# Seven block products for 20 of 22 up pairs in a split-precision FFN, with DMA-made weight sums in three buffers and tile addresses set by the kind of product

## The chip, the cores and the metric

The kernel runs on one core of a Trainium2 chip. The metric is the device time of one execution in microseconds (us), lower is better. A core has a matrix engine (TensorE, PE in the profile; its weight loads are listed as PEld), a vector engine (VectorE, DVE), an activation engine (ScalarE, ACT), a general engine (GpSimd, POOL) and a sync engine (SyncE, SP). They run their own instruction streams and meet through semaphores. Data lies in on-chip memory of 128 partitions, matmul results go to accumulation banks, and DMA queues move data; SP and POOL issue the DMAs spoken of here. "L398" is line 398 of the kernel before.

## The reference, cut to what matters

512 positions, width 1024, two layers. Layer 0 mixes tokens by causal pooling and a short convolution, layer 1 by gated linear attention; each layer then has a gated FFN with a convolution, and it is there that most of the change lies:

```python
def conv_ffn(h, w_up, conv_w, conv_b, w_down):
    u, v = jnp.split(h @ w_up, 2, axis=-1)          # 2816 channels each
    u = causal_dwconv(u, conv_w, conv_b)            # 3 taps over positions
    return (jax.nn.gelu(u, approximate=False) * v) @ w_down

def reference(x, ...):
    for l in range(DEPTH):                          # DEPTH = 2
        hn = rmsnorm(x, mix_norm[l])
        if l % 2 == 0:
            h = hn @ ab_w_in[i]
            ...                                     # pooling and short convolution
            y = jnp.concatenate([ya, yb], axis=-1) @ ab_w_out[i]
        else:
            y = gla_mixer(hn @ gla_w_in[i], ...) @ gla_w_out[i]
        x = x + y
        x = x + conv_ffn(rmsnorm(x, ffn_norm[l]), ffn_w_up[l], ffn_conv_w[l], ffn_conv_b[l], ffn_w_down[l])
    return rmsnorm(x, final_norm)
```

Inputs and output are float32.

## The kernel before

**Layout and precision.** Channels lie on the 128 partitions, the 512 positions along a row. Every float32 operand of a product is cut into a high and a low part by `split` (L136 on ACT makes the high part, L137 on DVE the low one), and every product is made in three passes: high by high, high by low, low by high. The normalized activations are held as eight tiles `xh[k]` and eight `xl[k]`. Weights come by DMA into raw tiles of 128x1024 (pool `wp`, four buffers of kind `raw`), and the parts into pool `wsp` (kinds `hi` and `lo`, four buffers each). For most weights `fetch` does load and split, one block ahead of use; `accumulate` (L219) then runs 8 matmuls of 512 columns for each pass.

**The stages.** In order: the input projection of layer 0 (pu, pc, px, pb by the program's names) and its mixer, the output projection abo, FFN up, FFN down (dn); then layer 1: a projection with the activations as the stationary operand (vg, L757 to L759, 256 columns), q, k and r, the attention, the output projection go, FFN up, FFN down. The last block of the last FFN down is made in two halves of 256 columns.

**FFN up** has 22 pairs in each layer; a pair is 128 channels of u and the 128 channels of v that they gate. `UP_KINDS` says how each pair is made:

- P, `plain`: two plain products, 2 x 3 passes x 8 = 48 matmuls of 512 columns (L398). The factor `rs` of the norm is multiplied in afterwards (L339). There are 6 P pairs per layer, at places 0, 1, 7, 13, 20 and 21.
- S, `seven`: the pair is seen as a 2x2 block product (u and v by the two halves of the 1024 inputs; those by the two halves of the 512 positions) and made with seven products in place of eight: p1 to p7, each 3 passes x 4 = 12 matmuls of 256 columns (L474), 84 in all, into the banks stx, sty and stz. There are 16 S pairs per layer.

The seven products need sums of blocks. On the activation side `mix_tokens` makes them once per layer (L341 to L360; the last of its additions is L352, and the parts are called th and tl). On the weight side each S pair makes them anew. The row of weights of a pair in memory is four quarters of 512: v.k1, v.k2, u.k1, u.k2.

- `load` issues three DMAs together, 12 units of the plan before the pair's start: L418 on SP brings v.k1 and v.k2 to a raw tile (raw left); L421 on SP brings u.k1 twice into a tile of kind `sum` (two buffers); L422 on POOL adds v.k1 to its first and u.k2 to its second half, with a DMA that accumulates. `load_right` (L426 on SP) brings u.k2 to the second half of another raw tile (raw right).
- `prep_a` splits raw left (a1). `prep_b` makes s2 (L443, DVE) from the sum's second half and v.k1, splits it (sh, sl), and makes a further difference, here called C (L445, DVE), from v.k2 and s2 into the first half of raw right. `prep_c` splits the sum (s31), `prep_d` raw right (a2).
- The products use them in this order: p1 and p2 read a1, p6 reads s2, p5 and p7 read s31, p4 and p3 read a2 (`LAYOUT`). On PE the p4 and p3 of a pair run among the products of the next one: p1, p2, p4 of the pair before, p6, p3 of the pair before, p5, p7.
- DVE and ACT take the results out of the banks (L483, L492, L505, L511, L516, L517), convolve over positions (`conv3`: L328 on ACT, L329 and L332 on DVE), and ACT applies the gelu.

**What sets the order.** `ffn_up` collects all its steps as events with a time in units (`at`): an S pair takes 7.0 units of this plan, a P pair 7.7 (`PERIOD`), and the sorted events are run. The framework then orders the instructions on each engine by its own estimates and inserts the semaphores: an instruction waits for the tiles that it reads and for the readers of the memory that it writes. SP's and POOL's issues go down their queues in their own order, and an issue that waits holds the ones behind it.

**Where tiles lie.** Single tiles of 128x512 come out of the pool `big` (`slot`, 46 buffers): u, v, the convolution's accumulators, s2, sh, sl, the gelu's results, y_h and y_l (parts of what abo and go read), vt (the attention's values) and mh and ml (parts of what FFN down reads). `xh` and `xl` are eight tiles each of 512 + 8 elements, of which 512 are used; the other tiles are 512 or 1024 elements with no gaps. The diagonal matrices of the norm (L265, DVE) feed matmuls (L276, L277) that spread the norm's factor; on PE they stand directly behind the first P pair, among the first products of the second pair.

Of the kernel before, what the change touches and what calls it, by code (L numbers as in the profile page):

```python
# [7 lines left out]
F32 = mybir.dt.float32  # L8
F32R = mybir.dt.float32r
I32 = mybir.dt.int32  # L10
AF = mybir.ActivationFunctionType
ALU = mybir.AluOpType

P = 128
T = 512
D = 1024
# [12 lines left out]
VG_COLS = (272, 256, 256, 256)  # L29
VG_K = ((3, 3, 2), (4, 4), (4, 4), (4, 4))  # L30
WBLK = 1024
NBIG = 46
AHEAD = 1
H = T // 2
HK = KD // 2
QUARTER = HK * P
UP_KINDS = "PPSSSSSPSSSSSPSSSSSSPP"
TILE_ORDER = (0, 4, 1, 5, 2, 6, 3, 7)
LAYOUT = {"p1": 0, "p2": 1, "p6": 3, "p5": 5, "p7": 6, "p4": 9, "p3": 11}
PERIOD = {"S": 7.0, "P": 7.7}  # L40
# [16 lines left out]
def trunk_kernel(ctx, tc, xT, cols, w_ab, w_pool, w_abo, w_vg, w_qkr, w_g2, w_go, w_up, w_dn, outT):  # L57
# [2 lines left out]

    cp = ctx.enter_context(tc.tile_pool(name="cp", bufs=1))
    big = ctx.enter_context(tc.tile_pool(name="big", bufs=NBIG))
    wp = ctx.enter_context(tc.tile_pool(name="wp", bufs=4))
    wsp = ctx.enter_context(tc.tile_pool(name="wsp", bufs=4))
    hp = ctx.enter_context(tc.tile_pool(name="hp", bufs=5))
    sp = ctx.enter_context(tc.tile_pool(name="sp", bufs=2))
# [1 line left out]

    def slot(dt=F32, name="s"):
        return big.tile([P, T], dt, tag="s", name=name)  # L70

    def half(name):
        return hp.tile([P, H], F32, tag="h", name=name)
# [4 lines left out]
    xall = cp.tile([P, KD * T], F32, tag="x", name="xall")  # L78
    x3 = xall.rearrange("p (k t) -> p k t", k=KD)
    x = [xall[:, k * T : (k + 1) * T] for k in range(KD)]  # L80
    xh = [cp.tile([P, T + 8], F32R, tag=f"xh{k}", name=f"xh{k}")[:, :T] for k in range(KD)]
    xl = [cp.tile([P, T + 8], F32R, tag=f"xl{k}", name=f"xl{k}")[:, :T] for k in range(KD)]
    colt = cp.tile([P, NCOLS], F32, tag="cols", name="colt")

    def col(name, i=0):
# [4 lines left out]
    for g in range(2):  # L90
        lead.append((
            wp.tile([P, WBLK], F32, tag="raw", name="raw_lead")[:, :D],
            wsp.tile([P, WBLK], F32R, tag="hi", name="hi_lead")[:, :D],
            wsp.tile([P, WBLK], F32R, tag="lo", name="lo_lead")[:, :D],
        ))

    def lead_load(g, part):
# [14 lines left out]
    for k in range(3, KD):  # L112
        x_load(k)

    ones = cp.tile([P, P], F32, tag="ones", name="ones")
    V.memset(ones, 1.0)
    ones_r = cp.tile([P, P], F32R, tag="ones_r", name="ones_r")
    V.tensor_copy(ones_r, ones)
    warm_in = sp.tile([P, 1], F32, tag="warm", name="warm_in", bufs=1)
    S.activation(warm_in, ones[:, 0:1], AF.Sqrt)  # L120
    warm = ps.tile([P, T], F32, tag="ps", name="warm")
# [17 lines left out]
    def weight_order():  # L139
        for g in range(2, 4):  # L140
            yield w_ab[g], KD, P
        for j in range(4):
            for b in (8 + j, 12 + j, 4 + j):
                yield w_ab[b], KD, P
        for j in TILE_ORDER:
            yield w_abo[j], KD, P
        for l in range(2):
            for j in range(NF):
                if UP_KINDS[j] == "P":
                    yield w_up[l, j, :, :D], KD, P  # L150
                    yield w_up[l, j, :, D:], KD, P
            for j in range(KD):
                k0 = 0
                for kt in DOWN_K:
                    yield w_dn[l, j, :, k0 * P : (k0 + kt) * P], kt, P
                    k0 += kt
            if l == 0:
                off = 0
                for n, ks in zip(VG_COLS, VG_K):
                    for kt in ks:  # L160
                        yield w_vg[:, off : off + kt * n], kt, n
                        off += kt * n
                for h in range(HEADS):
                    yield w_qkr[h], KD, P
                    yield w_qkr[4 + h], KD, P
                for i in range(8):
                    yield w_qkr[8 + i], KD, P
                for j in TILE_ORDER:
                    yield w_go[j], KD, P
# [5 lines left out]
    def fetch():  # L175
        nxt = next(order, None)
        if nxt is None:
            return
        fetched[0] += 1
        src, kt, n = nxt  # L180
        m = kt * n
        raw = wp.tile([P, WBLK], F32, tag="raw", name="raw")[:, :m]
        hi = wsp.tile([P, WBLK], F32R, tag="hi", name="hi")[:, :m]
        lo = wsp.tile([P, WBLK], F32R, tag="lo", name="lo")[:, :m]
        nc.sync.dma_start(raw, src)
        split(hi, lo, raw)
        ready.append([t.rearrange("p (k n) -> p k n", k=kt) for t in (hi, lo)])
# [172 lines left out]
    def ffn_up(l, rs, mixed):  # L360
# [12 lines left out]
        }  # L373
        ms = [None] * NF
        events = []

        def at(t, fn):
            events.append((t, len(events), fn))
# [33 lines left out]
        def seven(j, base):  # L412
            w, b, q = {}, {}, {}

            def load():
                src = w_up[l, j]
                w["raw", 0] = wp.tile([P, WBLK], F32, tag="raw", name="raw")
                nc.sync.dma_start(w["raw", 0], src[:, :D])  # L418
                s31 = w["s31"] = wp.tile([P, WBLK], F32, tag="sum", name="s31", bufs=2)
                s3 = s31.rearrange("p (a n) -> p a n", a=2)  # L420
                nc.sync.dma_start(s3, src[:, None, D : D + QUARTER].broadcast_to([P, 2, QUARTER]))  # L421
                G.dma_start(s3, src.rearrange("p (a n) -> p a n", a=4)[:, 0:4:3, :], accum_op=ALU.add)  # L422

            def load_right():
                w["raw", 1] = wp.tile([P, WBLK], F32, tag="raw", name="raw")
# [1 line left out]

            def parts(name, src, wide=True):
                if wide:
                    h = wsp.tile([P, WBLK], F32R, tag="hi", name="hi")  # L430
                    lo = wsp.tile([P, WBLK], F32R, tag="lo", name="lo")
                else:
                    h, lo = slot(F32R, "sh"), slot(F32R, "sl")
                split(h, lo, src)
                w[name] = (h, lo)

# [2 lines left out]

            def prep_b():  # L440
                r, c, s31 = w["raw", 0], w["raw", 1], w["s31"]
                s2 = slot(name="s2")
                V.scalar_tensor_tensor(s2, s31[:, QUARTER:], -1.0, r[:, :QUARTER], ALU.mult, ALU.subtract)  # L443
                parts("s2", s2, False)
                V.tensor_tensor(c[:, :QUARTER], r[:, QUARTER:], s2, ALU.subtract)  # L445
# [4 lines left out]
            def prep_d():  # L450
                parts("a2", w["raw", 1])

            at(base - 12, load)
            at(base - 9, load_right)
            at(base - 6, prep_a)
            at(base - 4, prep_b)
            at(base - 1, prep_c)
# [66 lines left out]

        def split_m(n):
            for j in range(len(mh), min(len(mh) + n, NF)):
                mh.append(slot(F32R, "mh"))
                ml.append(slot(F32R, "ml"))
                split(mh[j], ml[j], ms[j])

        base, item = 0.0, fetched[0] - len(ready)
        last_s = UP_KINDS.rindex("S")
        for j, kind in enumerate(UP_KINDS):
            if kind == "P":
                plain(j, base, item)
                item += 2
                if j > last_s + 1:
                    for i in range(5):
                        at(base + (i + 0.5) * PERIOD["P"] / 5, lambda: split_m(2))
            else:  # L540
                seven(j, base)
            base += PERIOD[kind]
# [55 lines left out]
    for k in range(KD):  # L598
        square_acc(k, acc)

    y_h = [slot(F32R, "yh") for _ in range(8)]
    y_l = [slot(F32R, "yl") for _ in range(8)]
    _, rs = norm_rows(acc, 1, 2)

# [72 lines left out]
    for i in range(2):  # L677
        G.memset(att_t[i], 0.0)

    vtok = [[slot(name="vt") for _ in range(2)] for _ in range(NTT)]  # L680
    gl = [sp.tile([P, STACK], F32, tag="gl", name="gl", bufs=4) for _ in range(NTT)]
    for c in range(NTT):
        G.memset(gl[c], 0.0)
# [336 lines left out]
```

## Time and profile before

| | us |
|---|---|
| time, median of 3 runs | 1082.23 (1081.52 to 1082.47) |
| the profiled execution's own time | 1081.95 |
| its span in the trace | 1080.2 |
| PE busy in the span | 1065.6 (99%) |
| DVE busy | 717.2 (66%) |
| ACT busy | 528.3 (49%) |
| POOL busy | 43.3 (4%) |

The span is what the trace covers, from the first to the last instruction; the execution's own time has 1.75 us more around it. Busy time is the sum of an engine's instructions, with overlaps counted once. A row for an instruction gives its start, its length, engine, line, operation, the tile written and those read, and their shape; several alike are put in one row with their number behind an x. The matmuls of a row overlap one another, so that the time of one is read from the starts of two rows divided by the number between them, not from its length. The groups of the page do not tell the shapes of a line apart unless they say so.

### The profile page before, as it was taken

Reading aid. Unit: us, or ns where it says so; the run is one execution under the profiler, and the core shown is the slowest. Engines: PE = TensorE matmul, PEld = TensorE weight load, DVE = VectorE, ACT = ScalarE, POOL = GpSimd, SP = SyncE. Lnnn points to the kernel's source line nnn. Section 1 sums busy time; section 2 is a strip of 40 time slices with the busy share of each in tenths; the row PEclk is TensorE's granted clock in tenths of the full one; section 3 lists DMA queues with packets and bytes.
Section 4 is the critical chain, followed back from the end, with each engine's and each line's share of the span. In section 5 each row is a group of like instructions: output and inputs, shape, how many; then the busy total and the mean of one; then the engine's idle time right before and its main releaser. Section 6 shows DMA issues by size and latency. Waiting matters only on the chain.

```text
span 1080.2 us, 15708 instructions
## 1 busy us (share of the span) xinstructions
PE 1065.6 (99%) x6298; PEld 940.7 (87%) x6298; DVE 717.2 (66%) x1060; ACT 528.3 (49%) x777; POOL 43.3 (4%) x71
## 2 busy tenths in 40 slices
PE   9999999999999999999999999999999999999995
PEld 6788889999999888889988888889999999888885
DVE  6786687879788663336455565677878798663324
ACT  6332555656566552224762354565656566552113
POOL 1000000101001000000000000000001010000000
PEclk9999999999999999999999999999999999999998
DMA  8521235857577433333232111235857575333302
GB/s 276 169 96 39 79 117 133 216 132 172 150 182 210 126 93 102 90 96 107 79 114 82 40 40 39 78 117 127 210 136 179 151 179 153 107 88 107 91 18 78
DMA packets 49289, 129.59 MB, mean 120 GB/s; under 512 B 4448, under 2 KB 6880, under 8 KB 49216
## 3 DMA queue, kind: packets, MB, share of 16 engines
q1 hardware_dynamic: 39280, 110.64, 33.3%
q0 software_dynamic: 8704, 16.78, 9.4%
q10 hardware_dynamic: 1232, 1.17, 0.3%
q8 instruction: 49, 0.80, 0.3%
q14 instruction: 24, 0.20, 0.1%
HBM read 126.48 MB, written 2.10 MB: 119 GB/s over the span
## 4 chain that ended last, share of the span: by engine, by line
PE 96%; DVE 1%; DMA 1%; ACT 1%; issue 0%; SPq 0%; DVEq 0%; ACTq 0%
PE dn L219 22%; PE stx L474 17%; PE stz L474 8%; PE u L398 6%; PE v L398 6%; PE sty L474 4%; PE r L219 4%; PE go L219 4%; PE abo L219 4%; PE k L219 2%; PE pb L219 2%; PE q L219 2%; PE pc L219 2%; PE px L219 2%; PE vg L759 1%; PE vg L757 1%
## 5 line engine op out<-in xcount | busy, mean ns | idle before, releaser
L136 ACT ACTIVATE hi<-raw 128x1024 fp32r<-128x1024 f32 (+2 forms) x191 | 198.0, 1037 | 248.3 <-PE dn L219 121.6
L137 DVE TENSOR_TENSOR lo<-raw,hi 128x1024 fp32r<-128x1024 f32 (+2 forms) x191 | 227.9, 1194 | 116.0 <-ACT hi L136 50.6
L219 PE MATMUL dn<-ml,hi 128*128 128x512 f32 (+1 forms) x374 | 89.4, 377 | 0.0
L219 PE MATMUL dn<-mh,hi 128*128 128x512 f32 (+1 forms) x374 | 89.3, 377 | 0.0
L219 PE MATMUL dn<-mh,lo 128*128 128x512 f32 (+1 forms) x374 | 88.6, 377 | 0.0
L219 PEld LDWEIGHTS dn<-mh,hi 128*128 128x128 f32 x374 | 67.7, 188 | 13.8 <-ACT mh L136 0.9
L219 PEld LDWEIGHTS dn<-mh,lo 128*128 128x128 f32 x374 | 67.7, 188 | 12.9
L219 PEld LDWEIGHTS dn<-ml,hi 128*128 128x128 f32 x374 | 67.7, 188 | 12.8
L422 POOL DMA_DIRECT2D s<-in_w_up x32 | 38.6, 1206 | 718.2 <-DVE cacc L408 248.8
L328 ACT ACTIVATE cacc<-u,colt 128x512 f32<-128x512 f32 x48 | 39.2, 816 | 53.5 <-DVE u L511 24.3
L234 ACT ACTIVATE xh<-xall,colt 128x512 fp32r<-128x512 f32 x32 | 22.9, 722 | 56.0 <-DVE xall L314 54.9
L483 ACT ACTIVATE k<-stx 128x256 f32<-128x256 f32 x96 | 35.6, 371 | 15.0 <-PE stx L474 15.0
L382 ACT ACTIVATE cacc<-cacc 128x512 f32<-128x512 f32 x44 | 27.8, 632 | 30.6 <-DVE cacc L332 30.6
L136 ACT ACTIVATE hi<-s 128x1024 fp32r<-128x1024 f32 x32 | 33.7, 1054 | 17.1 <-PE v L398 11.5
L329 DVE SCALAR_TENSOR_TENSOR cacc<-u,colt,cacc 128x511 f32<-128x511 f32 x48 | 35.8, 746 | 8.4 <-ACT cacc L328 8.4
L474 PE MATMUL stx<-th,lo 128*128 128x256 f32 x256 | 41.1, 283 | 0.0
L474 PE MATMUL stx<-tl,hi 128*128 128x256 f32 x256 | 41.0, 282 | 0.0
L474 PE MATMUL stx<-th,hi 128*128 128x256 f32 x256 | 40.9, 282 | 0.0
L137 DVE TENSOR_TENSOR lo<-s,hi 128x1024 fp32r<-128x1024 f32 x32 | 38.9, 1215 | 0.6 <-issue 0.6
L757 PE MATMUL vg<-hi,xh 128*128 128x256 f32 (+1 forms) x128 | 36.4, 284 | 0.0
L759 PE MATMUL vg<-lo,xh 128*128 128x256 f32 (+1 forms) x128 | 36.3, 283 | 0.0
L332 DVE SCALAR_TENSOR_TENSOR cacc<-u,colt,cacc 128x510 f32<-128x510 f32 x48 | 35.8, 745 | 0.6
(289 smaller groups left out, 2313.8 us busy)
## 6 DMA issues: line engine op xcount, KB each, us to landing
raw<-in_w_up SPq DMA_DIRECT2D x56, 512.0 KB, 4.6
s<-in_w_up SPq DMA_DIRECT2D x32, 512.0 KB, 5.5
s<-in_w_up POOLq DMA_DIRECT2D x32, 512.0 KB, 7.9
raw<-in_w_dn SPq DMA_DIRECT2D x32, 448.0 KB, 3.4
raw<-in_w_up SPq DMA_DIRECT2D x32, 256.0 KB, 3.2
raw<-in_w_dn SPq DMA_DIRECT2D x16, 512.0 KB, 3.6
raw<-in_w_qkr SPq DMA_DIRECT2D x16, 512.0 KB, 3.7
raw<-in_w_ab SPq DMA_DIRECT2D x14, 512.0 KB, 5.4
```

The source lines that it names most:

```text
L136: S.activation(hi, src, AF.Copy)
L137: V.tensor_tensor(lo, src, f32(hi), ALU.subtract)
L219: PE.matmul(out, w[:, k, :], a[k], start=first and i == 0 and k == 0, stop=last and i == 2 and k == n - 1)
L328: S.activation(acc, u, AF.Identity, bias=col(bname, j), scale=col(wname, 2 * nj + j))
L329: V.scalar_tensor_tensor(acc[:, 1:], u[:, : T - 1], col(wname, nj + j), acc[:, 1:], ALU.mult, ALU.add)
L332: V.scalar_tensor_tensor(acc[:, 2:], u[:, : T - 2], col(wname, j), acc[:, 2:], ALU.mult, ALU.add)
L398: PE.matmul(o, w[:, k, :], a[k], start=i == 0 and k == 0, stop=i == 2 and k == KD - 1)
L422: G.dma_start(s3, src.rearrange("p (a n) -> p a n", a=4)[:, 0:4:3, :], accum_op=ALU.add)
L474: PE.matmul(b[out][:, :H], wt[:, ks[k]], a[k], start=first and i == 0 and k == 0, stop=i == 2 and k == HK - 1, skip_group_check=True,)
L483: S.activation(q[name], b["x"][:, :H], AF.Copy)
L757: PE.matmul(o[c][:, :n], xh[kk][:, cs], h[:, k, :], start=kk == 0, stop=False)
L759: PE.matmul(o[c][:, :n], xh[kk][:, cs], lo[:, k, :], start=False, stop=kk == KD - 1)
```

## The change

What it does, part by part:

- `UP_KINDS` becomes one P pair, 20 S pairs and one P pair, in both layers.
- The raw tiles have three buffers (four before), the sums three (two before), in a pool of the FFN's up stage.
- `load` is taken apart: `load_sum` 17 units before the pair's start, `add_sum` 12.5, `load_left` 10 (raw left), and `load_right` 4.5 (9 before).
- s2 has no tile of its own: it is made in the first quarter of raw right's tile, where C is written afterwards.
- Two stage pools share one piece of memory. "side" holds y_h, vt, and the mh and ml of the last four pairs; "up" holds the sums, sh and sl. One is closed when the other is opened: "up" at the start of FFN up, "side" again 5.2 units into the last P pair.
- `big` has 41 buffers (46 before).
- `xh` and `xl` have no gap. Two gap tiles (48 and 40 elements) are put in, the hi and lo tiles are 64 elements wider, and the parts used lie 16 elements into them for S pairs and for the last block of the last FFN down, 48 for vg, 0 elsewhere. This sets the distance between the address of the columns that move through PE and that of the weights loaded next.
- Splits of mh and ml are begun during the last P pair.

```diff
-NBIG = 46
+WPITCH = WBLK + 64
+SKEW = 16
+VG_SKEW = 48
+NBIG = 41
+NSIDE = 8
-UP_KINDS = "PPSSSSSPSSSSSPSSSSSSPP"
+UP_KINDS = "PSSSSSSSSSSSSSSSSSSSSP"
-    wp = ctx.enter_context(tc.tile_pool(name="wp", bufs=4))
+    wp = ctx.enter_context(tc.tile_pool(name="wp", bufs=3))
+    stage = {}
+
+    def open_stage(name):
+        if "stack" in stage:
+            stage["stack"].close()
+        stage["stack"] = ctx.enter_context(ExitStack())
+        stage[name] = stage["stack"].enter_context(tc.tile_pool(name=name, bufs=NSIDE))
+
+    def side(dt=F32, name="s"):
+        return stage["side"].tile([P, T], dt, tag="s", name=name)
+
+    open_stage("side")
-    xh = [cp.tile([P, T + 8], F32R, tag=f"xh{k}", name=f"xh{k}")[:, :T] for k in range(KD)]
-    xl = [cp.tile([P, T + 8], F32R, tag=f"xl{k}", name=f"xl{k}")[:, :T] for k in range(KD)]
+    xh = [cp.tile([P, T], F32R, tag=f"xh{k}", name=f"xh{k}") for k in range(KD)]
+    xl = [cp.tile([P, T], F32R, tag=f"xl{k}", name=f"xl{k}") for k in range(KD)]
+    cp.tile([P, 48], F32, tag="gap", name="gap")
+    sp.tile([P, 40], F32, tag="gap", name="gap", bufs=1)
...
-                    yield w_dn[l, j, :, k0 * P : (k0 + kt) * P], kt, P
+                    yield w_dn[l, j, :, k0 * P : (k0 + kt) * P], kt, P, SKEW * (l == 1 and j == KD - 1)
-                        yield w_vg[:, off : off + kt * n], kt, n
+                        yield w_vg[:, off : off + kt * n], kt, n, VG_SKEW
-        src, kt, n = nxt
+        src, kt, n, *skew = nxt
+        part = slice(skew[0], skew[0] + m) if skew else slice(0, m)
-        hi = wsp.tile([P, WBLK], F32R, tag="hi", name="hi")[:, :m]
-        lo = wsp.tile([P, WBLK], F32R, tag="lo", name="lo")[:, :m]
+        hi = wsp.tile([P, WPITCH], F32R, tag="hi", name="hi")[:, part]
+        lo = wsp.tile([P, WPITCH], F32R, tag="lo", name="lo")[:, part]
...
+        open_stage("up")
...
-            def load():
-                src = w_up[l, j]
+            def load_sum():
+                s31 = w["s31"] = stage["up"].tile([P, WBLK], F32, tag="sum", name="s31", bufs=3)
+                src = w_up[l, j][:, None, D : D + QUARTER].broadcast_to([P, 2, QUARTER])
+                nc.sync.dma_start(s31.rearrange("p (a n) -> p a n", a=2), src)
+
+            def add_sum():
+                src = w_up[l, j].rearrange("p (a n) -> p a n", a=4)[:, 0:4:3, :]
+                G.dma_start(w["s31"].rearrange("p (a n) -> p a n", a=2), src, accum_op=ALU.add)
+
+            def load_left():
                 w["raw", 0] = wp.tile([P, WBLK], F32, tag="raw", name="raw")
-                nc.sync.dma_start(w["raw", 0], src[:, :D])
-                s31 = w["s31"] = wp.tile([P, WBLK], F32, tag="sum", name="s31", bufs=2)
-                s3 = s31.rearrange("p (a n) -> p a n", a=2)
-                nc.sync.dma_start(s3, src[:, None, D : D + QUARTER].broadcast_to([P, 2, QUARTER]))
-                G.dma_start(s3, src.rearrange("p (a n) -> p a n", a=4)[:, 0:4:3, :], accum_op=ALU.add)
+                nc.sync.dma_start(w["raw", 0], w_up[l, j, :, :D])
...
                 if wide:
-                    h = wsp.tile([P, WBLK], F32R, tag="hi", name="hi")
-                    lo = wsp.tile([P, WBLK], F32R, tag="lo", name="lo")
+                    h = wsp.tile([P, WPITCH], F32R, tag="hi", name="hi")[:, SKEW : SKEW + WBLK]
+                    lo = wsp.tile([P, WPITCH], F32R, tag="lo", name="lo")[:, SKEW : SKEW + WBLK]
                 else:
-                    h, lo = slot(F32R, "sh"), slot(F32R, "sl")
+                    h = stage["up"].tile([P, T + 64], F32R, tag="sh", name="sh", bufs=2)[:, SKEW : SKEW + T]
+                    lo = stage["up"].tile([P, T + 64], F32R, tag="sl", name="sl", bufs=2)[:, SKEW : SKEW + T]
...
-                s2 = slot(name="s2")
+                s2 = c[:, :QUARTER]
                 V.scalar_tensor_tensor(s2, s31[:, QUARTER:], -1.0, r[:, :QUARTER], ALU.mult, ALU.subtract)
                 parts("s2", s2, False)
                 V.tensor_tensor(c[:, :QUARTER], r[:, QUARTER:], s2, ALU.subtract)
...
-            at(base - 12, load)
-            at(base - 9, load_right)
+            at(base - 17, load_sum)
+            at(base - 12.5, add_sum)
+            at(base - 10, load_left)
+            at(base - 4.5, load_right)
             at(base - 6, prep_a)
             at(base - 4, prep_b)
             at(base - 1, prep_c)
...
-                mh.append(slot(F32R, "mh"))
-                ml.append(slot(F32R, "ml"))
+                make = side if j >= NF - NSIDE // 2 else slot
+                mh.append(make(F32R, "mh"))
+                ml.append(make(F32R, "ml"))
...
+                if j > last_s and not closed:
+                    closed = True
+                    at(base + 5.2, lambda: open_stage("side"))
-                if j > last_s + 1:
+                if j > last_s + 1 or j == NF - 1:
                     for i in range(5):
                         at(base + (i + 0.5) * PERIOD["P"] / 5, lambda: split_m(2))
...
-    y_h = [slot(F32R, "yh") for _ in range(8)]
+    y_h = [side(F32R, "yh") for _ in range(8)]
...
-    vtok = [[slot(name="vt") for _ in range(2)] for _ in range(NTT)]
+    vtok = [[side(name="vt") for _ in range(2)] for _ in range(NTT)]
```

## The prediction

> **What bounds the kernel now.** The page first: the engines' share, then the chain that ended last.
>
> ```profile
> PE 1065.6 (99%) x6298; PEld 940.7 (87%) x6298; DVE 717.2 (66%) x1060; ACT 528.3 (49%) x777; POOL 43.3 (4%) x71
> PE 96%; DVE 1%; DMA 1%; ACT 1%; issue 0%; SPq 0%; DVEq 0%; ACTq 0%
> ```
>
> PE is the bound everywhere, so only two things can save time: fewer columns through PE, or less time for each. For the second I read PE's rows in order of time and divide the distance between starts by the number of matmuls.
>
> ```profile
> 86.82 2.04 PE L219 MATMUL pc<-xh,hi 128*128 128x512 f32 x8
> 88.70 2.04 PE L219 MATMUL pc<-xl,hi 128*128 128x512 f32 x8
> ...
> 416.88 1.75 PE L219 MATMUL dn<-mh,hi 128*128 128x512 f32 x7
> 418.46 1.75 PE L219 MATMUL dn<-ml,hi 128*128 128x512 f32 x7
> ...
> 315.34 0.64 PE L474 MATMUL stx<-th,sh 128*128 128x256 f32 x4
> 315.82 0.64 PE L474 MATMUL stx<-tl,sh 128*128 128x256 f32 x4
> ...
> 531.32 0.28 PE L757 MATMUL vg<-hi,xh 128*128 128x256 f32 x1
> ...
> 531.66 0.28 PE L757 MATMUL vg<-hi,xh 128*128 128x256 f32 x1
> ```
>
> 512 columns take 1.88/8 = 235 ns in pc, but 1.58/7 = 226 in dn. 256 columns take 0.48/4 = 120 ns in an S product, but 0.34/3 = 113 in this stretch of vg. I laid these intervals beside the tiles' addresses, as the distance between moving columns and the weights loaded next, modulo 256 bytes. At 512 columns, distance 0 (abo, dn, go) gives 226.5; the products that read xh and xl, whose gaps spread them over eight distances, give 234.4 in the mean. At 256 columns it is the other way: vg gives 120.8 at distance 0 and 116 at 192 (114 in its even runs), 117 to 119 elsewhere; all S products together 119.2.
>
> Then one S pair from p1 to p1, in the table of engines by window, and its DVE rows.
>
> ```profile
> core 0: us, PE busy (x) PEld busy (x) DVE busy (x) ACT busy (x) POOL busy (x), PEclk, DMA share, GB/s
> 311.06:321.07 10.01, 10.01 (x87) 10.01 (x85) 9.10 (x14) 6.35 (x11) 1.20 (x1) 1.00 0.78 182
> ```
>
> ```profile
> 314.18 0.42 DVE L492 TENSOR_TENSOR v<-sty,k 128x256 f32<-128x256 f32 x1 [0.75 <-PE sty L474]
> 314.73 1.22 DVE L137 TENSOR_TENSOR lo<-raw,hi 128x1024 fp32r<-128x1024 f32 x1
> 315.96 0.69 DVE L511 TENSOR_TENSOR u<-u,rs 128x512 f32<-128x512 f32 x1
> 316.57 0.68 DVE L443 SCALAR_TENSOR_TENSOR s<-s,raw 128x512 f32<-128x512 f32 x1
> 317.29 0.69 DVE L445 TENSOR_TENSOR raw<-raw,s 128x512 f32<-128x512 f32 x1
> 317.90 0.74 DVE L329 SCALAR_TENSOR_TENSOR cacc<-u,colt,cacc 128x511 f32<-128x511 f32 x1
> 318.56 0.68 DVE L137 TENSOR_TENSOR sl<-s,sh 128x512 fp32r<-128x512 f32 x1
> 319.16 0.74 DVE L332 SCALAR_TENSOR_TENSOR cacc<-u,colt,cacc 128x510 f32<-128x510 f32 x1
> ```
>
> An S pair takes PE 10.01 us (a P pair 11.24), DVE 9.10 of it, DMA 0.78. DVE is the next bound, close behind. The last view is the start of the first up stage (first v at 147.4):
>
> ```profile
> 158.65 0.68 DVE L265 TENSOR_TENSOR diag<-ident,yl 128x512 fp32r<-128x512 f32 x1
> 159.67 0.40 PE L276 MATMUL bc<-diag,ones_r 128*128 128x512 f32 x1
> ```
>
> The norm's diagonal ends 0.34 us before PE wants it: no margin there.
>
> **The change part by part,** against the profiled execution's own 1081.95 (0.28 below the median, within its scatter).
>
> A. Eight P pairs become S: 8 x (11.24 - 10.01) = **-9.8**.
>
> B. 512-column products of xh and xl go to distance 0: 720 in pu, pc, px, pb, q, k, r and 192 in the four P pairs left, 912 x (234.4 - 226.5 = 7.9 ns) = **-7.2**.
>
> C. 256-column products go to distance 192: 40 x 84 + 192 in vg + 132 in the last dn block, 3684 x (119.2 - 116 = 3.2 ns) = **-11.8**. Ends: 114 gives -19.2, 120 gives +2.9. I take vg's mean at that distance. An S pair would then take PE 84 x 0.116 = 9.74.
> A rule against B and C stands in the Trainium skill, "SBUF — State Buffer", section "SBUF: two separate sides": the ports of PE, ACT and DVE's own pair wait for nobody, which leaves an address nothing to do; the sum would lack B and C. The rows of pc and dn contradict it for 512 columns.
>
> D. The two stage starts. In layer 1 the first sums lie in memory that y_h holds, which the last abo matmul reads at 147.6; before, their load went out at 12 us. A sum load takes 4.3 to 5.5 us to land and the POOL addition 0.56 later another 5.8 to 7.9, so the sum is there about 12 us into the stage. DVE's s2 and its split of that sum (0.68, 1.2) and ACT's of it stand ahead of the norm's short operations and the diagonal, a chain of 5.8 us: diagonal at about 17.8, PE wants it at 12: **+6**. In layer 2 the sums come early, but the second S pair's raw left waits for a buffer that the last operation of the activation sums (L352, 152.80 in layer 1, 5.8 us into the stage) releases; 3.9 to land, the same chain: about 15.8: **+4**. Ends: 0, if DVE's wait finds slack, and 14. An idle PE also loses its clock: in the window 1065 to 1070 it is 0.98, from 1070 on, with PE busy 1.22 of 5.00, 0.50. I add **+2** for a slower restart (ends 0 and 3.7).
> The Trainium skill, "TensorE: Matmul & The Clock Gate", halves the clock after an idle window of about 3.4 us and gives it back after as long a busy one; by it each restart would cost some 1.7 us, 3.4 in all, and no row here shows a recovery in mid-kernel.
>
> E. With three raw buffers a new loop appears. Raw left of a pair goes into the buffer of raw left of the pair before, which is free when C (L445) is done; s2 needs raw left and stands before C. In the changed order of DVE, s2 to the end of C holds, by starts of the rows: s2 0.60, L332 0.66, L516 0.34, a split 1.12, L517 0.60, sl 0.60, a split 1.14, L505 0.34, C 0.69: 6.09. With 0.08 for semaphores the loop is 6.17 + X, X being raw left's time to land. Before, X was 3.6 to 6.9 (median 4.4, beside the sum's load issued with it); alone 3.9. Now it is issued about 3.3 us after the sum's load and 1.7 before POOL's addition. I take X = 4.0, the quiet row: loop 10.17. DVE's own work alone would take 9.73 (8.77 back to back and 0.97 for ACT's convolution pass of 0.82, which now stands uncovered between L511 and L329), just under PE's 9.74. Queued behind the waiting s2 are the sum's split of the pair before, L517, sl and the next a1, so PE waits for p5 and p6. The pairs have a lead of about 4 us to lose; then some 15 pairs a layer run at the loop's pace: 2 x (15 x 0.43 - 4) = **+4.9**. Ends: 0 (X below 3.8) and 2 x (15 x 1.63 - 4) = +41 (X = 5.2).
>
> Costed at nothing: the sum's path, because its buffer now comes free 16.75 us before use and the path takes some 12 (5.5 + 0.56 + 5.8 = 11.9; it would bind above 16.75); SP's three issues of 0.33 to 0.38 and POOL's 1.20 per extra pair, behind waits that are long (POOL is at 4%); the three raw buffers in other stages (about 16.8 us between release and use, against 3.5 to 3.9 to land); 41 slots, since s2, sh, sl and eight y_h no longer need any; the splits of mh and ml at the stage's end (DVE has some 10 us of margin in dn). If these covers fail, PE idles before dn.
>
> Sum: 1081.95 - 9.8 - 7.2 - 11.8 + 10 + 2 + 4.9 = **1070**.
>
> **The rivals.**
> R1, slower: raw left lands late. What speaks for it: the median of 4.4 before, and landings of 4.7 to 6.9 when one was issued about 1 us after a POOL addition; against: 3.9 alone, and the sum's load is now mostly over. It is slower from X = 4.4 on (loop 10.57: 2 x (15 x 0.83 - 4) = 16.9, which uses up the rest of the sum, 1065.2 without E). At X = 5.0 the loop is 11.17: 2 x (15 x 1.43 - 4) = 35, so 1100.
> R2: S products stay at 119.2, because their operands change halves every four matmuls, as vg's do not. PE then takes 10.01 and E falls away: 1065.2 + 11.8 = 1077.
> R3: the stage starts cost nothing and the loop keeps under PE: 1065.2 - 12 = 1053. For it: after the stall, leads recover; against: the 0.34 us of margin.
> R4, the addresses do nothing at all (E then falls away too): 1081.95 - 9.8 + 12 = 1084. Against it the rows of pc and dn, unless other traffic made them differ. The page of the Trainium skill named under C would have it so.
>
> **How the numbers follow.** Forecast 0.41 (range of its own 1062 to 1078), R1 0.30, R2 0.15, R3 0.10, R4 0.04. A measurement of this kernel tells about 0.2% (2 us) from no change. Faster: the forecast, R3 and two thirds of R2, 0.61; the same 0.04, from R2 and R4; slower 0.35, R1 with what is left of those two. The range goes to just under R3, 1051, and to R1's price at X = 5.0, 1100.
>
> **What would show it.** 512-column intervals of 226 to 227 in pc and r (B); S products at about 116 and an S pair of 9.7 to 10.2 (C, E); PE idle just ahead of L276 at both up stages, ended by DVE's diagonal (D); in the S pairs DVE waiting at s2 for the DMA of raw left, and that DMA waiting on SP for C (E). An S pair above 10.57 makes it slower and me wrong; so do sums that land after s2 asks for them, or a wait of PE ahead of dn.

## The result, and the profile after

The changed kernel takes 1083.8 us in the median (1081.96 to 1087.94 in twelve executions; before 1081.59, 1081.52 to 1082.52). The ratio is 1.0026, with a 95% interval of 1.0013 to 1.0038: 2 us slower, just at the bound of what can be told from no change, where 1070 had been forecast. Single executions now scatter over 6 us, before over 1. The profiled execution is one of the fastest: 1081.99, span 1080.3.

The page after, its engines, then its chain (shares by engine, then by line):

```profile
PE 1047.6 (97%) x6586; PEld 937.4 (87%) x6586; DVE 741.1 (69%) x1116; ACT 543.4 (50%) x825; POOL 52.7 (5%) x79
PE 65%; DVE 16%; DMA 11%; issue 6%; ACT 2%; DVEq 0%; SPq 0%; ACTq 0%
PE dn L239 22%; DMA raw<-in_w_up 9%; PE stx L502 7%; PE r L239 4%; PE abo L239 4%; PE go L239 4%; DVE lo L156 3%; PE q L239 2%; PE k L239 2%; PE px L239 2%; PE pb L239 2%; PE stz L502 2%; DVE raw L469 2%; DVE cacc L352 2%; DVE cacc L545 2%
```

PE is busy 18 us less than before, in the same span. It no longer carries the whole chain (65% in place of 96%): a quarter of it now runs through DVE (16%) and through one kind of DMA, the load of raw left (9%). (Lines have moved: L419 is before's L398, L502 is L474, L469 makes s2, L471 makes C, L296 is L276, L285 the diagonal, L349 and L352 the convolution on DVE, L156 all the low parts.)

PE's rows in order of time, in pc, in an S pair and in vg:

```profile
86.06 1.98 PE L239 MATMUL pc<-xl,hi 128*128 128x512 f32 x8
87.88 1.98 PE L239 MATMUL pc<-xh,lo 128*128 128x512 f32 x8
...
247.83 0.62 PE L502 MATMUL stx<-th,sh 128*128 128x256 f32 x4
248.28 0.62 PE L502 MATMUL stx<-tl,sh 128*128 128x256 f32 x4
...
530.03 0.28 PE L789 MATMUL vg<-hi,xh 128*128 128x256 f32 x1
...
530.38 0.28 PE L789 MATMUL vg<-hi,xh 128*128 128x256 f32 x1
```

The addresses work. 512 columns take 1.82/8 = 227 ns in pc (235 before), 256 columns 0.45/4 = 113 in the S pair (120 before) and 0.35/3 = 117 by these rounded starts in vg; over the unrounded starts vg's 256-column products have 113 to 114 in nearly all groups. An S pair without a wait takes 84 x 113.3 = 9.52 us, less than the 9.74 reckoned.

The start of the up stage of layer 1 (first v at 144.29): DVE's rows, then PE's, then the engines by window (columns as in the prediction).

```profile
160.65 0.69 DVE L469 SCALAR_TENSOR_TENSOR raw<-s,raw 128x512 f32<-128x512 f32 x1 [8.82 <-DMA s<-in_w_up]
...
161.80 1.23 DVE L156 TENSOR_TENSOR lo<-s,hi 128x1024 fp32r<-128x1024 f32 x1 [0.38 <-ACT hi L155]
...
165.62 0.69 DVE L285 TENSOR_TENSOR diag<-ident,yh 128x512 fp32r<-128x512 f32 x1
166.22 0.68 DVE L285 TENSOR_TENSOR diag<-ident,yl 128x512 fp32r<-128x512 f32 x1
```

```profile
166.36 0.80 PE L296 MATMUL bc<-diag,ones_r 128*128 128x512 f32 x1 [9.81 <-DVE diag L285]
```

```profile
core 0: us, PE busy (x) PEld busy (x) DVE busy (x) ACT busy (x) POOL busy (x), PEclk, DMA share, GB/s
156.60:166.20 9.60, 0.00 (x0) 0.00 (x0) 5.17 (x11) 3.58 (x4) 1.20 (x1) 0.67 0.93 180
166.30:169.90 3.60, 3.54 (x14) 3.35 (x15) 2.54 (x5) 0.60 (x1) 1.19 (x1) 0.50 0.50 166
```

PE idles 9.81 us for the diagonal, which stands on DVE behind s2 and the split of a sum that is there only 16.3 us into the stage; then PE works 3.6 us at a granted clock of 0.50. In layer 2 the same wait is 2.90 us, again followed by some 3 us at 0.50.

Then the loop. In the late S pairs of the second layer, DVE's rows and the chain's step between them:

```profile
902.34 0.69 DVE L469 SCALAR_TENSOR_TENSOR raw<-s,raw 128x512 f32<-128x512 f32 x1 [0.54 <-DMA raw<-in_w_up]
...
907.75 0.68 DVE L471 TENSOR_TENSOR raw<-raw 128x512 f32<-128x512 f32 x1
...
913.27 0.69 DVE L469 SCALAR_TENSOR_TENSOR raw<-s,raw 128x512 f32<-128x512 f32 x1 [1.13 <-DMA raw<-in_w_up]
```

```profile
908.50 4.67 DMA raw<-in_w_up
```

s2 to the end of C is 6.09 us; 0.06 later the load of the next raw left goes out, lands after 4.67, and 0.10 later the next s2 starts: 10.93 from s2 to s2. This holds from the fifth pair of layer 1 and the seventh of layer 2 on, for 28 intervals: 6.25 + X to within 0.02 us, with X from 3.45 to 5.43 (mean 3.98), 10.23 in the mean, where PE needs 9.52. The group of s2 on the page, and one of PE's waits:

```profile
L469 DVE SCALAR_TENSOR_TENSOR raw<-s,raw 128x512 f32<-128x512 f32 x40 | 27.6, 691 | 27.5 <-DMA raw<-in_w_up 17.8
```

```profile
916.62 0.74 PE L502 MATMUL stx<-th,hi 128*128 128x256 f32 x4 [0.58 <-ACT k L511]
```

DVE stands idle for raw left. PE's waits in the S pairs all stand ahead of p7 (28 times) or of p4 (14 times, as here), and what ends each is ACT's copy of an earlier product out of the bank stx (L511). On ACT that copy stands behind operations that wait for DVE, such as the split of s2 (sh).

What the up stages hold, from the intervals between PE's matmuls: 458.0 us before (229.0 each), 468.2 after (235.7 and 232.4). Of these 425.9 are the work at the best intervals; 13.1 are waits ahead of L296, 21.3 waits within the S pairs, 4.3 S intervals at 118 in place of 113, and 3.6 the half clock. All else in the kernel is 10.1 shorter, 5.5 of it by the 512-column products.

### The profile page after: what moved, and what is told of

The parts are those of the page before. It is cut to its first block, busy times and chain, and to the rows that moved or that the text cites. A ratio compares the mean times of both kernels' runs of the same rounds, so it can differ in the third digit from the quotient of the medians.

```text
span 1080.3 us, 16455 instructions
## 1 busy us (share of the span) xinstructions
PE 1047.6 (97%) x6586; PEld 937.4 (87%) x6586; DVE 741.1 (69%) x1116; ACT 543.4 (50%) x825; POOL 52.7 (5%) x79
## 4 chain that ended last, share of the span: by engine, by line
PE 65%; DVE 16%; DMA 11%; issue 6%; ACT 2%; DVEq 0%; SPq 0%; ACTq 0%
PE dn L239 22%; DMA raw<-in_w_up 9%; PE stx L502 7%; PE r L239 4%; PE abo L239 4%; PE go L239 4%; DVE lo L156 3%; PE q L239 2%; PE k L239 2%; PE px L239 2%; PE pb L239 2%; PE stz L502 2%; DVE raw L469 2%; DVE cacc L352 2%; DVE cacc L545 2%
## 5 line engine op out<-in xcount | busy, mean ns | idle before, releaser
L156 DVE TENSOR_TENSOR lo<-raw,hi 128x1024 fp32r<-128x1024 f32 (+2 forms) x191 | 227.7, 1192 | 90.8 <-PE dn L239 50.5
L443 POOL DMA_DIRECT2D s<-in_w_up x40 | 48.2, 1205 | 696.1 <-DVE lo L156 219.3
L502 PE MATMUL stx<-th,hi 128*128 128x256 f32 x320 | 55.0, 294 | 8.0 <-ACT k L511 7.1
L349 DVE SCALAR_TENSOR_TENSOR cacc<-u,colt,cacc 128x511 f32<-128x511 f32 x48 | 36.0, 751 | 35.4 <-ACT cacc L348 35.4
L502 PEld LDWEIGHTS stx<-th,hi 128*128 128x128 f32 x320 | 42.8, 188 | 16.0 <-ACT k L511 15.1
L502 PE MATMUL stx<-tl,hi 128*128 128x256 f32 x320 | 49.7, 278 | 0.0
L502 PE MATMUL stx<-th,lo 128*128 128x256 f32 x320 | 49.7, 278 | 0.0
L156 DVE TENSOR_TENSOR lo<-s,hi 128x1024 fp32r<-128x1024 f32 x40 | 48.7, 1217 | 0.6 <-ACT hi L155 0.6
L155 ACT ACTIVATE hi<-s 128x1024 fp32r<-128x1024 f32 x40 | 41.9, 1048 | 9.9 <-DMA s<-in_w_up 9.3
L469 DVE SCALAR_TENSOR_TENSOR raw<-s,raw 128x512 f32<-128x512 f32 x40 | 27.6, 691 | 27.5 <-DMA raw<-in_w_up 17.8
L502 PEld LDWEIGHTS stx<-tl,hi 128*128 128x128 f32 x320 | 42.7, 188 | 0.0
L502 PEld LDWEIGHTS stx<-th,lo 128*128 128x128 f32 x320 | 42.6, 188 | 0.0
L511 ACT ACTIVATE k<-stx 128x256 f32<-128x256 f32 x120 | 40.6, 366 | 2.5 <-PE stx L502 2.4
```

Source lines behind the costliest of these rows:

```text
L155: S.activation(hi, src, AF.Copy)
L156: V.tensor_tensor(lo, src, f32(hi), ALU.subtract)
L349: V.scalar_tensor_tensor(acc[:, 1:], u[:, : T - 1], col(wname, nj + j), acc[:, 1:], ALU.mult, ALU.add)
L443: G.dma_start(w["s31"].rearrange("p (a n) -> p a n", a=2), src, accum_op=ALU.add)
L502: PE.matmul(b[out][:, :H], wt[:, ks[k]], a[k], start=first and i == 0 and k == 0, stop=i == 2 and k == HK - 1, skip_group_check=True,)
L511: S.activation(q[name], b["x"][:, :H], AF.Copy)
```

## The experiments

The theory after the result: three costs ate the gain of A, B and C, namely the loop through raw left, DVE's order at the stage starts, and S intervals that do not always reach 113. Its rivals: the DMA traffic of twenty S pairs binds whatever the order; or the costs are the sums' path through POOL.

**s2 in a tile of its own.**

```diff
-                s2 = c[:, :QUARTER]
+                s2 = slot(name="s2")
```

> One line is undone: s2 gets a tile of its own again, so that C no longer waits for sl and stands on DVE directly behind s2, as in the kernel before. Three raw buffers, the DMAs and the addresses stay. Theory (the loop s2 - C - load of raw left binds the S pairs at a mean of 10.2 us, while their 84 matmuls need 9.52): the loop shrinks to about 1.3 us plus the load, S pairs take 9.5 to 9.6, which gives back 2 x 19 x 0.65 = some 20 to 25 us less the 4 to 6 that the first pairs never lost; in layer 2 the norm's diagonal now stands ahead of the second s2, so its stall of 3.3 us and the slow clock behind it go too; in layer 1 the split of the first sum still stands ahead of the diagonal and the stall of 10 us stays. About 1056 us (1050 to 1064). Rival (the DMA traffic of twenty S pairs, or the sums' path through POOL, binds): S pairs stay at 10.1 to 10.3 and the time at 1078 to 1084.

Measured: 1060.27 (1056.72 to 1065.43), ratio 0.9806 (0.9776 to 0.9837). DVE's rows of one S pair, and the group of s2:

```profile
323.03 0.68 DVE L469 SCALAR_TENSOR_TENSOR s<-s,raw 128x512 f32<-128x512 f32 x1
323.75 0.69 DVE L471 TENSOR_TENSOR raw<-raw,s 128x512 f32<-128x512 f32 x1
324.36 0.74 DVE L349 SCALAR_TENSOR_TENSOR cacc<-u,colt,cacc 128x511 f32<-128x511 f32 x1
```

```profile
L469 DVE SCALAR_TENSOR_TENSOR s<-s,raw 128x512 f32<-128x512 f32 x40 | 27.4, 684 | 0.0
```

C is back behind s2, none of the forty s2 waits, and from the fifth pair of each layer on PE has no wait. The same DMAs run in less time, so the traffic rival falls. Unlooked for: in the profiled execution (1065.43, the slowest of the four) layer 1 runs its S pairs in 9.52 us and layer 2 in 9.89, with no wait in either from the fifth pair on; the 256-column intervals are 118 ns there.

**Four raw buffers.**

```diff
-NBIG = 41
+NBIG = 39
-    wp = ctx.enter_context(tc.tile_pool(name="wp", bufs=3))
+    wp = ctx.enter_context(tc.tile_pool(name="wp", bufs=4))
```

> Raw tiles get four buffers again (39 slots in place of 41 to make room); s2 stays in place, C stays behind sl. Theory: a load of raw left then waits for a buffer that was free a pair earlier, so the loop is cut at the other end: S pairs 9.5 to 9.7; both stage starts still have s2 ahead of the diagonal, so their stalls (10.2 and 3.3 us in the changed kernel) stay. About 1064 us (1057 to 1070). Rival (in-place s2 costs by DVE's order alone, not by the buffers): S pairs stay above 10, 1078 to 1085. If the traffic binds, the same.

Measured: 1077.02 (1073.98 to 1080.69), ratio 0.996 (0.9944 to 0.9976). A miss: 7 us above the range expected. The loop through raw left is cut, but S pairs still take 10.3. Lines of the chain in layer 1:

```profile
201.95 1.15 DVE lo L156
203.11 4.94 DMA s<-in_w_up
208.61 7.27 DMA s<-in_w_up
```

The split of a sum (lo) ends, 0.03 us later the load of the third next sum goes into its tile, and POOL's addition follows 0.56 after the landing; s2 starts 0.09 after that has landed, in every steady pair. (The addition shown landed at 216.59; the chain counts its last 0.7 us as issue.) From load to s2 it is 12 to 16 us, and the split ends some 7 us behind the s2 two pairs earlier: about 20.7 for two pairs, 10.3 each. The order of DVE moves with the buffers: the split of a sum ends 6.9 us behind an s2 here and 2.8 in the changed kernel, so its buffer comes free later, and the sums' path binds in place of raw left. So the sums' rival holds for this kernel and not for the changed one, where s2 waited for raw left; and DVE's order, the rival of this expectation, has a part in it.

**The change without the addresses.** The tiles keep their places, all skews are 0, and xh and xl have their 8 elements again:

```diff
-WPITCH = WBLK + 64
-SKEW = 16
-VG_SKEW = 48
+WPITCH = WBLK
+SKEW = 0
+VG_SKEW = 0
-    xh = [cp.tile([P, T], F32R, tag=f"xh{k}", name=f"xh{k}") for k in range(KD)]
+    xh = [cp.tile([P, T + 8], F32R, tag=f"xh{k}", name=f"xh{k}")[:, :T] for k in range(KD)]
...
```

> All of the change but the addresses: xh and xl have their gaps of 8 elements again, the parts start at 0 in all tiles; the order on every engine is that of the changed kernel. Theory (in the S pairs the gain of the addresses is eaten by the loop): 512-column products of xh and xl go back to 234 ns, 912 x 7.7 = +7; the 256-column ones go back to about 119 ns and an S pair needs 10.0 of PE, which lies just under the loop's 10.2, so that only the first 4 or 5 pairs of a layer and vg lose something: +4 to +8. About 1096 us (1092 to 1100). Rival (savings simply add): 3684 x 5.9 = +21.7 with the 7 of the others, 1112. Rival (the addresses do nothing): 1084.

Measured: 1093.61 (1092.6 to 1097.9), ratio 1.0123 (1.01 to 1.0146). S pairs take 10.01 us, and 10.2 to 11.5 where the loop binds. So the addresses are worth 9.8 us in the changed kernel (1093.6 - 1083.8), a third of the 28 that their intervals save on PE (7.0 for 512 columns, 21.2 for 256). Most of the rest is found in the profiles: PE's waits in the up stages are 34 us with the addresses and 24 without, and 4.3 go into S intervals at 118. It is the clearest sign that the terms do not add.

**The kinds of before, all else of the change.**

```diff
-UP_KINDS = "PSSSSSSSSSSSSSSSSSSSSP"
+UP_KINDS = "PPSSSSSPSSSSSPSSSSSSPP"
```

> Kinds of the kernel before (16 S and 6 P pairs per layer), all else of the change. Theory: no S run is longer than six pairs, and its lead (about 4 us) is won back in a P pair, so the loop hardly shows; in layer 1 the diagonal stands ahead of s2 again, since the first S pair comes a pair later. From the time before: -10.0 (1296 products of 512 columns) - 15.9 (32 x 84 x 5.9 ns) - 1.5 (vg, last block) = 1054.5, plus 0 to 10 for what is left of loop and starts: 1055 to 1064, so 20 to 28 us faster than the changed kernel although it does 1.8% more columns. Rival (the loop costs the same per S pair however long the run): 32 x 0.65 = 21 more, about 1075.

Measured: 1074.71 (1070.91 to 1076.84), ratio 0.9932 (0.991 to 0.9954). A miss: the changed kernel is 9 us faster with 16 S pairs than with 20, where 20 to 28 were expected. The time is the rival's (about 1075), but not its mechanism, a cost that is the same in every S pair. The group of s2:

```profile
L469 DVE SCALAR_TENSOR_TENSOR raw<-s,raw 128x512 f32<-128x512 f32 x32 | 22.1, 691 | 40.1 <-DMA raw<-in_w_up 40.1
```

DVE's s2 waits for raw left in 28 of 32 pairs. The up stages hold 17.7 us of PE's waits and 5.8 of slow S intervals; in layer 1 the waits are largest in the first S pair behind each P pair (2.6, 2.7 and 2.2 us), so P pairs do not win the lead back.

**The diagonal first,** on top of s2's own tile:

```diff
-            at(base - 17, load_sum)
-            at(base - 12.5, add_sum)
+            at(base - 17 if j == 1 else max(base - 17, 1), load_sum)
+            at(base - 12.5 if j == 1 else max(base - 12.5, 2.5), add_sum)
...
-            at(base - 1, prep_c)
+            at(base - 1 + (3 if j == 1 else 0), prep_c)
```

> On top of the run with s2's own tile: the first S pair's split of its sum is planned 3 units later and the sums of the later pairs are asked for a little later, so that in both layers the norm's diagonal stands on DVE ahead of everything that needs a sum, and the first sum does not share its way with two others. The steady order of the S pairs is the same. Theory (the stall ahead of the norm's matmuls is DVE's order behind a late sum): the 5.8 us of idle ahead of L296 in layer 1 go; p6 of the first pair then waits for its sum instead, some 2 to 4 us: 1060.3 - 3 to - 7, so 1053 to 1058. Rival (PE would have waited the same time for the sum anyway): 1058 to 1062.

Measured: 1051.49 (1049.49 to 1059.13), ratio 0.9731 (0.9695 to 0.9767). PE at the start of layer 1's up stage:

```profile
156.66 0.39 PE L296 MATMUL bc<-diag,ones_r 128*128 128x512 f32 x1
...
164.12 1.22 PE L502 MATMUL stx<-th,sh 128*128 128x256 f32 x4 [4.09 <-ACT k L511]
```

L296 no longer waits. PE waits at p6 (stx from sh) instead, for 4.09 us; ACT, which takes a copy ahead of it, and DVE stand behind the first sum. So the rival is right for most of layer 1's stall: it was moved and not removed. The waits of layer 1's stage fall from 9.0 to 6.0 us and those of layer 2's from 4.0 to 2.8, and the half clock costs 2.3 less. The largest part of the 14.0 us between the two profiled executions (1065.43 and 1051.44) is another: layer 2 has its S pairs at 9.52 too, which is 7.2. The medians lie 8.8 apart, and how much of that is the order alone is not shown. The same kernel a second time:

> The kernel with s2's own tile and the diagonal first once more, on the same chip as the run with the kinds of before, with more rounds: 1051 to 1055 in the median, single executions up to 1060 where a layer's S pairs run at 118 ns.

Measured: 1052.91 (1051.67 to 1055.05), ratio 0.9733 (0.9719 to 0.9746). It is faster than the kernel before and than the changed one.

**The intervals by themselves.** This kernel leaves the computation out; in its place PE runs bursts of matmuls on x:

```diff
+    for n, count in ((256, 84), (512, 48)):
+        for rep in range(4):
+            for d in range(8):
+                o = ps.tile([P, T], F32, tag="ps", name=f"at{32 * d}b")
+                off = 8 * (-d % 8)
+                for i in range(count):
+                    w0 = off + (i % 32) * P
+                    m0 = (i % KD) * T
+                    PE.matmul(o[:, :n], left[:, w0 : w0 + P], moving[:, m0 : m0 + n], start=i == 0, stop=i == count - 1)
+                S.activation(seen[:, : 32 + 48 * rep + 4 * d], o[:, : 32 + 48 * rep + 4 * d], AF.Copy)
```

> The computation is left out: x is loaded and stored, and in between PE runs bursts of matmuls on it, 84 of 256 columns or 48 of 512, with nothing else running, at eight distances (0 to 224 bytes, modulo 256) of the moving columns from the weights loaded next, four bursts for each with a pause of changing length before it. Theory (the distance alone sets the interval): 512 columns 226 ns at 0 and 232 to 238 elsewhere; 256 columns 113 at 192, 120 to 121 at 0, 117 to 120 elsewhere; at 192 some of the four bursts may run at 118, which the S pairs of layer 2 showed after a stall. Rival (other engines' or DMA traffic makes the difference): the same interval at all distances, near 216 and 109.

PE's rows; one row is one burst, the name tells the distance:

```profile
37.30 9.79 PE L81 MATMUL at64b<-moving,left 128*128 128x256 f32 x84 [0.36 <-ACT seen L82]
...
79.21 9.80 PE L81 MATMUL at192b<-moving,left 128*128 128x256 f32 x84 [0.36 <-ACT seen L82]
...
99.95 10.34 PE L81 MATMUL at0b<-moving,left 128*128 128x256 f32 x84 [0.37 <-ACT seen L82]
...
163.70 10.17 PE L81 MATMUL at192b<-moving,left 128*128 128x256 f32 x84 [0.40 <-ACT seen L82]
...
450.01 11.18 PE L81 MATMUL at0b<-moving,left 128*128 128x512 f32 x48 [0.37 <-ACT seen L82]
461.57 11.45 PE L81 MATMUL at32b<-moving,left 128*128 128x512 f32 x48 [0.39 <-ACT seen L82]
473.41 11.27 PE L81 MATMUL at64b<-moving,left 128*128 128x512 f32 x48 [0.39 <-ACT seen L82]
...
520.65 11.46 PE L81 MATMUL at192b<-moving,left 128*128 128x512 f32 x48 [0.40 <-ACT seen L82]
```

With no other engine and no DMA beside a burst, the distance still sets the interval: the traffic rival falls here as well. (All weights of a burst lie at one distance, so it does not tell the weights loaded next from those in use.) Medians: 512 columns 227 at distance 0, 229 at 64 (not expected), 231 to 237 elsewhere; 256 columns 120 at 0, 117 to 121 at 32, 96, 128, 160 and 224. At 64 and 192 there are two values: a whole burst runs at 113 (9.80 us) or at 118 (10.17); at each of the two distances one burst of four took the faster. Both times it was the first, behind the shortest of the four pauses (0.36 us); whether the pause decides was not tried.

**Only xh and xl in the kernel before.**

```diff
-    xh = [cp.tile([P, T + 8], F32R, tag=f"xh{k}", name=f"xh{k}")[:, :T] for k in range(KD)]
-    xl = [cp.tile([P, T + 8], F32R, tag=f"xl{k}", name=f"xl{k}")[:, :T] for k in range(KD)]
+    xh = [cp.tile([P, T], F32R, tag=f"xh{k}", name=f"xh{k}") for k in range(KD)]
+    xl = [cp.tile([P, T], F32R, tag=f"xl{k}", name=f"xl{k}") for k in range(KD)]
...
+    cp.tile([P, 48], F32, tag="gap", name="gap")
```

> The kernel before, with one part of the change: xh and xl without their gaps, and one gap tile so that all distances are 0. The order on every engine is that of the kernel before. Theory (the parts add where PE is the bound, as it is there): 1296 products of 512 columns go from 234.3 to 226.7 ns = -9.8; the 256-column products of xh and xl go to distance 0, 120 in place of 119.2 and vg 120.8: +2 to +3. Net 1081.5 - 7 = 1074 to 1075. Rival (addresses do nothing, the gain seen elsewhere is of other origin): 1081.5.

Measured: 1077.11 (1076.61 to 1078.44), ratio 0.9957 (0.9941 to 0.9974). Term B alone, less what the 256-column products lose at distance 0 (120.0 in the S pairs): the direction holds, the gain is 4.9 where 7 was expected. u and v came to about 228 ns rather than 226.7.

**Kinds of before, with s2's own tile.** The two edits of the first and the fourth experiment together:

```diff
-UP_KINDS = "PSSSSSSSSSSSSSSSSSSSSP"
+UP_KINDS = "PPSSSSSPSSSSSPSSSSSSPP"
...
-                s2 = c[:, :QUARTER]
+                s2 = slot(name="s2")
```

> The run with s2's own tile (not the one with the diagonal first), with the kinds of the kernel before: 16 S and 6 P pairs. It tells what twenty S pairs are worth by themselves (term A), once nothing waits for a sum or a raw left. Theory: PE alone sets the time, 1081.6 - 10.0 (512 columns) - 15.9 (32 S pairs from 10.01 to 9.52) - 1.5 (vg, last block) = 1054, with no stall at the stage starts, because the first S pair comes a pair later; where S pairs run at 118 ns instead of 113 after a disturbance, each costs 0.37 more, so 1054 to 1064. The kernel with twenty S pairs and the diagonal first needs 8 x (10.87 - 9.52) = 10.8 less of PE and loses some 9 to 10 in its stage starts: the two come out within 5 us of each other. Rival (three raw buffers still bind where P pairs take them too, as in the run with these kinds and s2 in place): 1068 to 1075.

Measured: 1069.02 (1067.21 to 1069.16), ratio 0.9877 (0.9864 to 0.9891), a miss by 5. PE in an S pair:

```profile
250.55 0.64 PE L502 MATMUL stx<-th,hi 128*128 128x256 f32 x4
251.02 0.64 PE L502 MATMUL stx<-tl,hi 128*128 128x256 f32 x4
```

0.47/4 = 118 ns, in all 32 S pairs: 9.89 each, not one at 9.52. No S pair has a wait; the only wait is 2.3 us ahead of L296 in layer 1. 32 x 0.37 = 11.8 and these 2.3 on 1054 give 1068. So the rival (buffers) falls, although the time lies in its range. What twenty S pairs are worth by themselves is not cleanly shown: the run with s2's own tile, which differs in the kinds alone, is 8.8 us faster (1060.3), the one that also has the diagonal first 16 (1052.9). Of either, 10.8 are fewer columns; the rest hangs on the interval that the S pairs ran at, 118 or 113 (up to 12 us here), and on the stage starts.

## Why the prediction was wrong

The time lies in the forecast's range (1051 to 1100), on the other side of the kernel before: no gain of 12, but 2 us lost. That it lies in the range is partly luck: the range reaches so far up for a raw left that lands late, and it did not. The rival that came nearest in kind is R1, whose place is right and whose condition is not: raw left lands on average in 3.98, not above 4.4. R4's 1084 is the measured time by luck alone: the addresses do work.

- **A** (-9.8) rests on PE's need and was measured only together with other things (the last experiment). Nothing speaks against it.
- **B** (-7.2): 912 products at 226.6 to 227 instead of 234.4, -7. Right.
- **C** (-11.8) was too small: the interval is 113.3, outside the lower end of 114 given for it. PE's need falls by 21.2 in the S pairs, vg and the last block; 4.3 is lost again where S pairs run at 118. The rule that the Trainium skill, "SBUF — State Buffer", section "SBUF: two separate sides", gives (PE's ports wait for nobody) does not decide here: with nothing else running, the distance moved the interval by 4% at 512 columns and 7% at 256. R2 and R4 fall with the measured intervals.
- **D** (+10 and +2 for the clock): place, cause and order were right. Layer 1 cost 10.0 rather than 6: the first sum is there 16.3 us into the stage, not 12, since POOL's addition took 10.67 where 5.8 to 7.9 had been reckoned. It leaves beside four loads of SP (144.48 to 146.72), which is probably why. Layer 2 cost 3.1 rather than 4. The half clock cost 3.6 rather than 2: 1.9 behind the first idle and 1.7 behind the second. The estimate of 3.4 from the Trainium skill, "TensorE: Matmul & The Clock Gate", agrees with that; its idle window of about 3.4 us does not, since the second idle was only 2.90.
- **E** (+4.9) is the step that failed. Its loop was right to 0.1 us: 6.25 + X against 6.17 + X, 10.23 in the mean against 10.17. Its comparison was not: "The pairs have a lead of about 4 us to lose" and PE's 9.74. PE needed 9.52, and it waits from the fifth pair of layer 1 and the fourth of layer 2 on, so there was next to no lead left; that the lead had gone into the stalls of D is likely and not shown. 28 x (10.23 - 9.52) = 19.9, and the waits in the S pairs are 21.3. Where PE waits was also off: at p7 and p4, for ACT's copies, and not at p5 and p6.

The terms with their measured sizes, against 1081.95: A -9.8, B -7.0, C -21.2 + 4.3, D +13.1 + 3.6, E +21.3, and -2.0 for the last norm's sums at the end (4.6 us of PE time there, 6.6 before): 1084.3 against the profiled 1081.99. The rest, -2.3, was not followed. The deeper error is in the adding: C and E were two terms of a sum, but where a loop of 10.2 binds, whatever C takes off PE comes back in E. Had C been exactly as reckoned, E would still have been 28 x (10.23 - 9.74) = 14, not 4.9: that part is the missing lead.

R3 (no stalls, loop covered, 1053) is nearly what the kernel becomes by two small edits: 1052.9, with 8.8 us of waits left in the two stages and a faster interval than R3 reckoned with. What was not seen beforehand is that one line, s2 in place, made both the loop and, by the run that undoes it, half of the stalls ahead of L296 (13.1 to 5.9 us): C must wait for sl, and the planned order of DVE then puts six more instructions between s2 and C and moves s2 ahead of the diagonal.

## What to carry to other kernels

Before adding up a saving on the bounding engine, write down every loop of buffer, load and release beside it, with its period; a saving counts only down to the longest of them, and those terms are a maximum and not a sum. A tile reused in place is a wait: look at what its reader now holds back, on the engine's own queue and through the load that refills the buffer. When a buffer is added against one loop, the next one may bind at nearly the same period (here the sums', 10.3 us in place of 10.2).

## What the runs showed of the hardware

- The interval of these matmuls (fp32r parts) depends on the distance of the moving columns from the weights, modulo 256 bytes, with all other engines idle: at 512 columns 227 ns at 0 and up to 237 elsewhere; at 256 columns 120 at 0.
- At distances 64 and 192, 256-column matmuls have two stable intervals, 113.3 and 118 ns. A run of them keeps the one it has, for all the S pairs of a layer where nothing disturbs it: 9.52 or 9.89 us a pair. After waits they were found in either. What chooses between them is open. It may be, with X's scatter, why most of the kernels with the change scatter by 5 to 10 us between executions; forty S pairs at 0.37 would make 15. Of one kernel alone, the one with the diagonal first, two executions have a trace (1051.44 and 1052.91), and both have nearly all S pairs at 113.3, so this is argued and not shown.
- After stalls of 9.81 and 2.90 us in the middle of the changed kernel, PE ran 3.6 and some 3 us at a granted clock of 0.50. With the kinds of before a wait of 1.98 was followed by the same (0.50 from 830.3 to 833.6), and without the addresses one of 2.72 was not (1.00 from 739.1 on): the length of the idle does not decide alone.
- POOL's accumulating DMA of 512 KB took 5.8 to 10.0 us in the kernel before and 6.0 to 9.1 in the changed one, save the first, which left beside four loads of SP and took 10.7.
